# The value pass of a product-key expert layer, rewritten as one pipeline of columns with a pinned order

## The chip, the cores and the metric

One core of a Trainium2 chip runs one program. The metric is the device time of one execution in microseconds (us), taken as the median of several executions. The engines are TensorE (PE, with its weight loads shown apart as PEld), VectorE (DVE), ScalarE (ACT), GpSimd (POOL) and SyncE (SP). In this kernel nearly every transfer is issued by SP, from one queue, in the order in which the program puts them there.

## The reference, cut to what matters

The network has two layers. Each is a mixer (convolution, mLSTM and differential attention over 256 context and 256 latent tokens) followed by an expert layer with 16384 experts. The expert layer of a block of tokens is

```python
s = einsum(q(t), sub_keys); st, it = top_k(s, 16)          # two halves of the key
cand = st[..., 0, :, None] + st[..., 1, None, :]           # 16 x 16 sums, again top 16
g = softmax(best)                                          # gate of each chosen expert
u = take(eu, e, axis=0)
act = gelu(einsum("thkd,td->thk", u, t))
out = einsum("thk,thkd->td", g * act, take(ev, e, axis=0))
```

The kernel doesn't gather experts. It computes gelu(u t) for all 16384 experts, spreads the gates into a dense matrix G (zero for experts not chosen), and sums (G * act) times ev over all experts. The second half of that, the sum with ev, is the value pass.

## The kernel before, in words

The experts of a layer are 128 columns of 128. `peer` (L873) runs two phases. In the first, `route` finds and spreads the gates and writes them to DRAM (`G`), while `inner` (L851) computes the activations of a column: it loads `u`, splits it into a rounded part `uh` and a rest `ul`, runs the products on PE, takes the gelu (`ga`, L870) and stores that to DRAM (`act`). In layer 0 (512 tokens, so 512 activations per expert column and partition) all 128 columns are done there, since `NPRE[0]` is 128; in layer 1 (256 tokens) 104 of them are.

The second phase is `outer`, the value pass. Here is what one column of layer 0 costs:

- `weights` (L927): every fourth column loads the gate tile `g` (1 MB, L931) for four columns; every column loads its activations `gb` (256 KB, L937); DVE multiplies them (L943, in place), ACT rounds the product to `wh` (L946), DVE takes the rest `wl` (L947). It is called for two columns at a time.
- `values` (L952): loads the column's `v` (512 KB, L954); `usplit` splits it into two halves of `vh` (ACT, L846) and `vl` (DVE, L847).
- `second` (L957): 24 products of 128x128 by 128x512 on PE: for 4 blocks of 128 tokens and 2 halves of the 1024 outputs, `wh*vh` (L969), `wh*vl` (L970) and `wl*vh` (L971), summed over all columns in the 8 PSUM banks `acc`.
- one step of `side`, a generator that computes layer 1's modulation meanwhile: `wa` (512 KB, L177) is loaded every second column, and DVE multiplies it twice with a row-sum (`wtr`, L180).

The last column ends with `finish` (L975) for each bank: transposes, the residual and the statistics of the next norm, from which layer 1's front part follows.

What orders the work: the program is recorded and then a scheduler of the framework puts each engine's instructions, and SP's transfers, in an order of its own by its cost estimates; the semaphores follow from the buffers. A buffer of a tile name (its tag) is taken again only after everything that read it is done. The numbers of buffers for layer 0 are

```python
UB = (5, 8); UR = (2, 4)    # uh, ul: 5 each; u: 2
VB = (5, 6); VR = (2, 3)    # vh, vl: 5 each (halves of a column); v: 2
AB = (6, 4)                 # gb: 6;  wh, wl: 4 each;  g: 2;  wa: 2
```

Only the `wtr` steps are pinned (`keep_in_program_order`): pinned instructions of an engine keep the order in which the program names them, among themselves. All of PE's 3072 products of the value pass stand in the same order in any case, column by column.

The functions that the change touches, and what calls them:

Of the kernel before, what the change touches and what calls it, by code (L numbers as in the profile page):

```python
# [7 lines left out]
F32 = mybir.dt.float32  # L8
F32R = mybir.dt.float32r
# [3 lines left out]
AF = mybir.ActivationFunctionType  # L13
# [3 lines left out]
D = 1024  # L17
# [7 lines left out]
TG = 32  # L25
TT = 512
NPRE = (128, 104)
RATE = (((1, 3), (5, 8)), ((1, 2), (9, 8)))
UB = (5, 8)
UR = (2, 4)  # L30
VB = (5, 6)
VR = (2, 3)
AB = (6, 4)
# [17 lines left out]
class Net:  # L51
# [865 lines left out]
    def outer(self, l, P, h, c0, npre, Gd, Ad, pool, X, S, side):  # L917
        nc, I = self.nc, self.I
        n = TT - c0
        per = 512 // n  # L920
        nt = n // 128
        V = I["peer_v"][l].rearrange("(i j) d -> i j d", j=128)
        bank = lambda k: self.psum.tile([128, 512], F32, name=f"acc{k}", tag=f"acc{k}", bufs=1)
        acc = [bank(k) for k in range(2 * nt)]
        st = {}

        def weights(n2):  # L927

            if n2 % 2 == 0:
                st["g"] = X.tile([128, n // TG, 4, TG], F32, name="g", tag="g")  # L930
                nc.sync.dma_start(st["g"], Gd[:, :, 2 * n2:2 * n2 + 4, :])  # L931
            r = []
            for m in range(2 // per):
                bank = n2 * (2 // per) + m
                if bank * per < npre:
                    a = X.tile([128, 512], F32, name="gb", tag="gb", bufs=AB[l])
                    nc.sync.dma_start(a, Ad[bank])  # L937
                else:
                    a = st.pop(("a", bank))
                j4 = (bank * per) % 4  # L940
                av = a.rearrange("p (j a b) -> p j a b", j=per, b=TG)
                g = st["g"][:, :, j4:j4 + per, :].rearrange("p a j b -> p j a b")
                nc.vector.tensor_mul(av, av, g)  # L943
                wh = X.tile([128, 512], F32R, name="wh", tag="wh", bufs=2 * (2 // per))
                wl = X.tile([128, 512], F32R, name="wl", tag="wl", bufs=2 * (2 // per))
                nc.scalar.activation(wh, a, AF.Copy)  # L946
                nc.vector.tensor_sub(wl, a, wh)  # L947
                for k in range(per):
                    r.append((wh[:, k * n:(k + 1) * n], wl[:, k * n:(k + 1) * n]))
            st["w", n2] = r  # L950
# [6 lines left out]
        def second(n2):  # L957
            ws = st.pop(("w", n2))
            for jj in range(2):
                vs = values(2 * n2 + jj)  # L960
                wh, wl = ws[jj]
                s0, s1 = n2 == first and jj == 0, n2 == last and jj == 1
                order = (2, 0, 3, 1) if s1 and nt > 2 else range(nt)
                for tt in order:
                    t = slice(tt * 128, tt * 128 + 128)
                    for k in range(2):
                        A = acc[2 * tt + k]
                        vh, vl = vs[k]
                        nc.tensor.matmul(A, wh[:, t], vh, start=s0, stop=False)  # L969
                        nc.tensor.matmul(A, wh[:, t], vl, start=False, stop=False)  # L970
                        nc.tensor.matmul(A, wl[:, t], vh, start=False, stop=s1)  # L971
                        if s1:
                            finish(tt, k)
# [45 lines left out]
        early, late, seq = list(range(npre // 4)), list(range(npre // 4, 32)), []  # L1019
        for k in range(32):  # L1020
            q = late if not early or late and (k + 1) * (32 - npre // 4) // 32 > k * (32 - npre // 4) // 32 else early
            seq += [2 * q[0], 2 * q.pop(0) + 1]
        first, last = seq[0], seq[-1]
        for k in range(65):
            if k == 64:
                for _ in side:
                    pass
                self.log_exp(self.gelu)
            if k < 64:
                n2 = seq[k]  # L1030
                for j in (2 * n2, 2 * n2 + 1):
                    if j >= npre:
                        a = self.inner(l, h, c0, j, per, pool, S, nc.vector)
                        if a is not None:
                            st["a", j // per] = a
                weights(n2)
                next(side, None)
            if k:
                second(seq[k - 1])
            next(side, None)  # L1040


    def run(self):
# [110 lines left out]
```

## Time and profile before

| what | us |
|---|---|
| median of 3 executions (lowest to highest) | 3059.82 (3053.89 to 3063.95) |
| the profiled execution, its own time | 3061.33 |
| its span, first to last instruction | 3059.2 |
| TensorE busy / granted clock (share of full) | 2912.0 / 0.979 |
| VectorE, ScalarE, GpSimd busy | 2013.9, 1424.9, 1077.3 |
| value pass of layer 0, first product to the first product of its last column | 1227.3 to 1965.58 |

Times within the execution count from the first instruction of the span. A row of the view by groups gives line, engine, operation, tiles, count, busy time, mean ns, and the idle time of the engine just before with what ended it. A row of the view of waits gives who waited for whom, the total, how many times and the longest. Lines are those of the kernel before.

### The profile page before, as it was taken

To read this page: it belongs to the slowest core of one execution; us is meant where nothing else is said; L and a number is where in the kernel's file an instruction comes from. 1 tells how busy PE (TensorE), PEld (TensorE's weight loads), DVE (VectorE), ACT (ScalarE), POOL (GpSimd) and SP (SyncE) were. 2 spreads that over 40 slices of the span, in tenths; PEclk is the share of its full clock that TensorE was granted. 3 is DMA by queue.
4 is the path that set the end of the run, shared out by engine and by line. 5 is a ranking of instruction groups with operands and counts; after the bars stand their busy time and mean duration, and the time that the engine had idled before them with its cause. 6 is when DMAs were issued, how large, how long until landed. Compare 5 with 4: busy or idle time off the path is not lost.

```text
span 3059.2 us, 43325 instructions
## 1 busy us (share of the span) xinstructions
PE 2912.0 (95%) x14960; PEld 2407.3 (79%) x14960; DVE 2013.9 (66%) x4447; ACT 1424.9 (47%) x2862; POOL 1077.3 (35%) x887
## 2 busy tenths in 40 slices
PE   7899999999999999999999999988989999999998
PEld 4575578878888888887777777777689999888887
DVE  4856547865666665666665665486749788666665
ACT  4354443345665664332232223345455766555454
POOL 4333255656666665000000000054478877100000
PEclk9898899999999999999999999989999999999999
DMA  6521134445555556766766666221255877898773
GB/s 230 186 63 35 41 115 135 124 138 188 187 202 184 203 193 236 263 220 223 232 221 217 215 216 208 78 80 56 62 170 165 263 267 278 301 312 268 256 237 127
DMA packets 257868, 565.62 MB, mean 185 GB/s; under 512 B 18336, under 2 KB 119200, under 8 KB 254448
## 3 DMA queue, kind: packets, MB, share of 16 engines
q1 hardware_dynamic: 256928, 560.42, 54.5%
q8 instruction: 118, 1.93, 0.3%
q0 software_dynamic: 720, 2.43, 0.2%
q14 instruction: 102, 0.84, 0.1%
HBM read 464.21 MB, written 98.57 MB: 184 GB/s over the span
## 4 chain that ended last, share of the span: by engine, by line
PE 59%; DMA 13%; DVE 10%; issue 2%; ACT 2%; POOL 1%; SPq 0%; DVEq 0%; ACTq 0%; POOLq 0%
PE h L864 10%; PE h L866 10%; PE h L865 10%; DMA gb<-act 8%; PE acc L970 6%; PE acc L971 6%; PE acc L969 6%; DMA v<-in_peer_v 3%; PE f L813 3%; DVE vl L847 2%; DVE wl L947 1%; DVE cy L468 1%; PE f L311 1%; PE f L312 1%; DMA u<-in_peer_u 1%
## 5 line engine op out<-in xcount | busy, mean ns | idle before, releaser
L847 POOL TENSOR_TENSOR ul<-u,uh 128x512 fp32r<-128x512 f32 x464 | 611.6, 1328 | 335.4 <-ACT uh L846 317.3
L864 PE MATMUL h<-hh,uh 128*128 128x512 f32 (+1 forms) x2048 | 692.2, 338 | 3.8 <-ACT ga L870 3.8
L866 PE MATMUL h<-hh,ul 128*128 128x512 f32 (+1 forms) x2048 | 689.4, 337 | 5.2 <-POOL ul L847 5.1
L865 PE MATMUL h<-hl,uh 128*128 128x512 f32 (+1 forms) x2048 | 689.6, 337 | 0.0
L970 PE MATMUL acc<-vl,wh 128*128 128x512 f32 x1536 | 607.3, 396 | 28.6 <-DVE vl L847 27.5
L846 ACT ACTIVATE vh<-v 128x512 fp32r<-128x512 f32 x512 | 307.0, 626 | 660.9 <-DMA v<-in_peer_v 482.9
L969 PE MATMUL acc<-vh,wh 128*128 128x512 f32 x1536 | 598.5, 390 | 1.9 <-ACT vh L846 1.2
L971 PE MATMUL acc<-vh,wl 128*128 128x512 f32 x1536 | 599.2, 390 | 0.1
L846 ACT ACTIVATE uh<-u 128x512 fp32r<-128x512 f32 x512 | 319.1, 629 | 466.9 <-PE h L865 339.8
L847 DVE TENSOR_TENSOR vl<-v,vh 128x512 fp32r<-128x512 f32 x512 | 344.1, 687 | 171.4 <-ACT vh L846 171.0
L866 PEld LDWEIGHTS h<-hh,ul 128*128 128x128 f32 x2048 | 389.2, 190 | 47.1 <-POOL ul L847 6.3
L864 PEld LDWEIGHTS h<-hh,uh 128*128 128x128 f32 x2048 | 389.5, 190 | 45.2 <-ACT ga L870 5.7
L865 PEld LDWEIGHTS h<-hl,uh 128*128 128x128 f32 x2048 | 389.6, 190 | 37.0
L815 DVE TENSOR_REDUCE rt_stg<-f 128x256 f32<-128x512 f32 x384 | 245.0, 687 | 224.4 <-PE f L813 223.7
L970 PEld LDWEIGHTS acc<-vl,wh 128*128 128x128 f32 x1536 | 288.6, 188 | 114.9 <-DVE vl L847 57.3
L969 PEld LDWEIGHTS acc<-vh,wh 128*128 128x128 f32 x1536 | 288.8, 188 | 63.4 <-ACT vh L846 1.4
L971 PEld LDWEIGHTS acc<-vh,wl 128*128 128x128 f32 x1536 | 288.9, 188 | 58.2 <-DVE wl L947 0.6
L219 POOL TENSOR_TENSOR wlo<-wt,whi 128x512 fp32r<-128x512 f32 x164 | 231.4, 1422 | 253.4 <-ACT whi L218 230.1
L943 DVE TENSOR_TENSOR gb<-gb,g 128x512 f32<-128x512 f32 x180 | 126.0, 703 | 254.9 <-DMA gb<-act 252.2
L375 POOL MEMSET up<- 128x60 f32 (+1 forms) x2 | 0.3, 148 | 764.6 <-PE acc L991 764.6
L801 DVE SCALAR_TENSOR_TENSOR rt_oh_g<-iotap,rt_sT,rt_sg 128x256 fp32r<-128x256 f32 x512 | 213.4, 475 | 0.1
L218 ACT ACTIVATE whi<-wt 128x512 fp32r<-128x512 f32 x164 | 100.1, 626 | 140.6 <-PE f L298 52.2
(311 smaller groups left out, 4201.6 us busy)
## 6 DMA issues: line engine op xcount, KB each, us to landing
u<-in_peer_u SPq DMA_DIRECT2D x256, 512.0 KB, 4.0
v<-in_peer_v SPq DMA_DIRECT2D x256, 512.0 KB, 4.7
G<-rt_stg SPq DMA_DIRECT2D x24, 2048.0 KB, 6.7
act<-ga SPq DMA_DIRECT2D x180, 256.0 KB, 2.9
gb<-act SPq DMA_DIRECT2D x180, 256.0 KB, 4.8
g<-G SPq DMA_DIRECT2D x32, 1024.0 KB, 5.7
wa<-in_ada_t SPq DMA_DIRECT2D x56, 512.0 KB, 5.7
w<-in_ada_w SPq DMA_DIRECT2D x20, 1024.0 KB, 6.0
```

The costliest lines, as they stand in the source:

```text
L219: nc.gpsimd.tensor_sub(lo, raw, hi)
L801: nc.vector.scalar_tensor_tensor(og[:, k], self.iotap[:, None, :].to_broadcast([128, 2, 128]), sT[:, 1, c:c + 1], sg[:, c, :, None].bitcas ...
L815: nc.vector.tensor_reduce(stg[:, :, t4 + k2:t4 + k2 + 2].rearrange("p j t -> p t j"), pg.rearrange("p (t x j) -> p t j x", t=2, x=2), axis ...
L846: nc.scalar.activation(hi, raw[:, k * 512:(k + 1) * 512], AF.Copy)
L847: lo_eng.tensor_sub(lo, raw[:, k * 512:(k + 1) * 512], hi)
L864: nc.tensor.matmul(o, uh, hh[:, c, c0:], start=c == 0, stop=False)
L865: nc.tensor.matmul(o, uh, hl[:, c, c0:], start=False, stop=False)
L866: nc.tensor.matmul(o, ul, hh[:, c, c0:], start=False, stop=c == NB - 1)
L943: nc.vector.tensor_mul(av, av, g)
L969: nc.tensor.matmul(A, wh[:, t], vh, start=s0, stop=False)
L970: nc.tensor.matmul(A, wh[:, t], vl, start=False, stop=False)
L971: nc.tensor.matmul(A, wl[:, t], vh, start=False, stop=s1)
```

## The change

For layer 0 (`npre == 128`) `outer` now calls a new function, `outer_ahead`, and returns; layer 1 keeps the old code. The new function treats the 128 columns one by one. In the turn of column i it issues, in this order: the gate and activation loads of columns i+6 and i+7 (`gates`, every second turn), the load of v of column i+3 (`raw`), the split of column i+1 (`parts`), the rounding of the weights of column i+2 (`weight`), the gate product of column i+3 (`gated`), one step of `side`, and then the 24 products of column i. From the third turn on all of these but the products and the steps of `side` are pinned (the `wtr` of `side` were pinned before), so DVE, ACT and SP keep this order. v and its halves of odd columns live in the buffers of u, which are free by then, so there are 4 buffers of v where there were 2, and 10 each of vh and vl where there were 5. Counts of instructions, sizes and tiles of products are the same.

```diff
@@ -1021,6 +1021,9 @@
             q = late if not early or late and (k + 1) * (32 - npre // 4) // 32 > k * (32 - npre // 4) // 32 else early
             seq += [2 * q[0], 2 * q.pop(0) + 1]
         first, last = seq[0], seq[-1]
+        if npre == 128:
+            self.outer_ahead(l, seq, first, last, st, X, pool, Gd, Ad, V, acc, finish, side)
+            return
         for k in range(65):
             if k == 64:
                 for _ in side:
@@ -1038,6 +1041,105 @@
             if k:
                 second(seq[k - 1])
             next(side, None)
+
+    def outer_ahead(self, l, seq, first, last, st, X, pool, Gd, Ad, V, acc, finish, side):
+
+
+        nc = self.nc
+        cols = [2 * n2 + jj for n2 in seq for jj in range(2)]
+        hold = [False]
+
+        def pin(ins):
+            if hold[0]:
+                self.tc.keep_in_program_order(ins)
+            return ins
+
+        def gates(i):
+
+            if i >= len(seq):
+                return
+            n2 = seq[i]
+            if n2 % 2 == 0:
+                st["g", n2 // 2] = X.tile([128, TT // TG, 4, TG], F32, name="g", tag="g")
+                pin(nc.sync.dma_start(st["g", n2 // 2], Gd[:, :, 2 * n2:2 * n2 + 4, :]))
+            for j in (2 * n2, 2 * n2 + 1):
+                st["a", j] = X.tile([128, 512], F32, name="gb", tag="gb", bufs=AB[l])
+                pin(nc.sync.dma_start(st["a", j], Ad[j]))
+
+        def raw(i):
+            if i >= len(cols):
+                return
+            p, name = ((X, "v"), (pool, "u"))[i % 2]
+            v = st["v", i] = p.tile([128, D], F32, name="v", tag=name, bufs=(VR if i % 2 == 0 else UR)[l])
+            pin(nc.sync.dma_start(v, V[:, cols[i], :]))
+
+        def parts(i):
+            if i >= len(cols):
+                return
+            p, name, n = ((X, "v", VB), (pool, "u", UB))[i % 2]
+            v, r = st.pop(("v", i)), []
+            for k in range(2):
+                hi = p.tile([128, 512], F32R, name="vh", tag=name + "h", bufs=n[l])
+                lo = p.tile([128, 512], F32R, name="vl", tag=name + "l", bufs=n[l])
+                pin(nc.scalar.activation(hi, v[:, k * 512:(k + 1) * 512], AF.Copy))
+                pin(nc.vector.tensor_sub(lo, v[:, k * 512:(k + 1) * 512], hi))
+                r.append((hi, lo))
+            st["p", i] = r
+
+        def gated(i):
+
+            if i >= len(cols):
+                return
+            j = cols[i]
+            av = st["a", j].rearrange("p (a b) -> p a b", b=TG)
+            pin(nc.vector.tensor_mul(av, av, st["g", j // 4][:, :, j % 4, :]))
+
+        def weight(i):
+            if i >= len(cols):
+                return
+            a = st.pop(("a", cols[i]))
+            wh = X.tile([128, 512], F32R, name="wh", tag="wh", bufs=4)
+            wl = X.tile([128, 512], F32R, name="wl", tag="wl", bufs=4)
+            pin(nc.scalar.activation(wh, a, AF.Copy))
+            pin(nc.vector.tensor_sub(wl, a, wh))
+            st["w", i] = wh, wl
+
+        for i in range(3):
+            gates(i)
+            if i < 2:
+                raw(i)
+        raw(2)
+        gated(0)
+        gated(1)
+        weight(0)
+        parts(0)
+        gated(2)
+        weight(1)
+        for i in range(len(cols)):
+            hold[0] = i > 1
+            if i == len(cols) - 1:
+                for _ in side:
+                    pass
+                self.log_exp(self.gelu)
+            if i % 2 == 0:
+                gates(i // 2 + 3)
+            raw(i + 3)
+            parts(i + 1)
+            weight(i + 2)
+            gated(i + 3)
+            next(side, None)
+            (wh, wl), vs = st.pop(("w", i)), st.pop(("p", i))
+            s0, s1 = i == 0, i == len(cols) - 1
+            for tt in (2, 0, 3, 1) if s1 else range(4):
+                t = slice(tt * 128, tt * 128 + 128)
+                for k in range(2):
+                    A = acc[2 * tt + k]
+                    vh, vl = vs[k]
+                    nc.tensor.matmul(A, wh[:, t], vh, start=s0, stop=False)
+                    nc.tensor.matmul(A, wh[:, t], vl, start=False, stop=False)
+                    nc.tensor.matmul(A, wl[:, t], vh, start=False, stop=s1)
+                    if s1:
+                        finish(tt, k)
 
 
     def run(self):
```

VectorE, in the steady part of the pass. `gb` is a column's activations (number by buffer), `vl` the rest of v, `wl` the rest of the weights. First the kernel before, from the half split of one column to the gate product of a column six later than the first `wl` here (`gb_11899` takes the buffer that `wl_11635` frees by reading `gb_11631`):

```order
L847 TENSOR_TENSOR vl_11654<-v_11647,vh_11653 128x512
L947 TENSOR_TENSOR wl_11635<-gb_11631,wh_11634 128x512
L847 TENSOR_TENSOR vl_11684<-v_11681,vh_11683 128x512
L847 TENSOR_TENSOR vl_11688<-v_11681,vh_11687 128x512
L947 TENSOR_TENSOR wl_11642<-gb_11638,wh_11641 128x512
L180 SCALAR_TENSOR_TENSOR wtr_11645,red_11448<-wa_11627,cb_11440 128x1024
L180 SCALAR_TENSOR_TENSOR wtr_11717,red_11448<-wa_11715,cb_11440 128x1024
L847 TENSOR_TENSOR vl_11740<-v_11737,vh_11739 128x512
L943 TENSOR_TENSOR gb_11899<-gb_11899,g_11897 128x512
```

The same engine in the change, two turns of it (`gb_11650` takes the buffer of `gb_11440`, which was last read five turns before; `v_11695` takes the buffer of `v_11516`, split four turns before):

```order
L1095 TENSOR_TENSOR gb_11562<-gb_11562,g_11560 128x512
L180 SCALAR_TENSOR_TENSOR wtr_11712,red_11531<-wa_11710,cb_11484 128x1024
L1085 TENSOR_TENSOR vl_11747<-v_11654,vh_11746 128x512
L1085 TENSOR_TENSOR vl_11751<-v_11654,vh_11750 128x512
L1104 TENSOR_TENSOR wl_11755<-gb_11562,wh_11754 128x512
L1095 TENSOR_TENSOR gb_11564<-gb_11564,g_11560 128x512
L180 SCALAR_TENSOR_TENSOR wtr_11759,red_11531<-wa_11710,cb_11484 128x1024
L1085 TENSOR_TENSOR vl_11788<-v_11695,vh_11787 128x512
L1085 TENSOR_TENSOR vl_11792<-v_11695,vh_11791 128x512
L1104 TENSOR_TENSOR wl_11796<-gb_11564,wh_11795 128x512
L1095 TENSOR_TENSOR gb_11650<-gb_11650,g_11560 128x512
L180 SCALAR_TENSOR_TENSOR wtr_11802,red_11531<-wa_11800,cb_11484 128x1024
```

What moved: each turn is now split, split, `wl`, gate product, `wtr`, once each; before, gate products and `wtr` came in pairs between the splits. The gate product that stood seven rows behind the `wl` that frees its buffer now stands 26 rows behind it.

SP's transfers in the kernel before (`v_11771` takes the buffer of `v_11681`, two columns earlier):

```order
L954 DMA v_11737<-in_peer_v 128x1024
L937 DMA gb_11899<-act0_2986 128x512
L954 DMA v_11771<-in_peer_v 128x1024
L937 DMA gb_11906<-act0_2986 128x512
L177 DMA wa_11805<-in_ada_t 128x1024
L954 DMA v_11825<-in_peer_v 128x1024
L937 DMA gb_11987<-act0_2986 128x512
L954 DMA v_11859<-in_peer_v 128x1024
L937 DMA gb_11994<-act0_2986 128x512
```

SP's transfers in the change:

```order
L1067 DMA gb_11650<-act0_2986 128x512
L177 DMA wa_11710<-in_ada_t 128x1024
L1067 DMA gb_11652<-act0_2986 128x512
L1074 DMA v_11654<-in_peer_v 128x1024
L1074 DMA v_11695<-in_peer_v 128x1024
L1064 DMA g_11738<-G0_2985 128x16x128
L1067 DMA gb_11740<-act0_2986 128x512
L177 DMA wa_11800<-in_ada_t 128x1024
L1067 DMA gb_11742<-act0_2986 128x512
L1074 DMA v_11744<-in_peer_v 128x1024
```

What moved: the two `v` of a pair now stand together, behind the `gb` loads, four columns after the split that frees their buffers where it was two; `wa` and `g` keep their places between them.

ScalarE where the pass begins, in the kernel before (`uh` is the split of the last u columns, `ga` their gelu):

```order
L870 ACTIVATE ga_11288<-h_11255 128x512
L946 ACTIVATE wh_11429<-gb_11426 128x512
L946 ACTIVATE wh_11436<-gb_11433 128x512
L946 ACTIVATE wh_11456<-gb_11453 128x512
L846 ACTIVATE uh_11374<-u_11367 128x512
L846 ACTIVATE vh_11471<-v_11469 128x512
L846 ACTIVATE vh_11475<-v_11469 128x512
```

The same place in the change:

```order
L870 ACTIVATE ga_11288<-h_11255 128x512
L1103 ACTIVATE wh_11448<-gb_11426 128x512
L1103 ACTIVATE wh_11461<-gb_11428 128x512
L1084 ACTIVATE vh_11452<-v_11430 128x512
L1084 ACTIVATE vh_11456<-v_11430 128x512
L846 ACTIVATE uh_11374<-u_11367 128x512
L1103 ACTIVATE wh_11479<-gb_11432 128x512
```

What moved: the two halves of the first column of v come ahead of the last half of the last u (`uh_11374`). PE and POOL keep their order throughout, and on every engine the instructions of `finish` and those behind it stand in the same order in both. One `wtr` that the scheduler had put into the phase before (at 441.9 us) now stands in the pass.

## Rows read from the trace of the kernel before

**Rows 1.** Page: busy time of the engines; shares of the chain that ended last.

```profile
PE 2912.0 (95%) x14960; PEld 2407.3 (79%) x14960; DVE 2013.9 (66%) x4447; ACT 1424.9 (47%) x2862; POOL 1077.3 (35%) x887
PE 59%; DMA 13%; DVE 10%; issue 2%; ACT 2%; POOL 1%; SPq 0%; DVEq 0%; ACTq 0%; POOLq 0%
```

**Rows 2.** Two stretches, L970 alone: length, PE and PEld busy, clock, DMA share, GB/s.

```profile
1227.30:1379.70 152.40, 87.11 (x224) 42.04 (x224) 1.00 0.72 241
1379.70:1965.50 585.80, 317.30 (x793) 148.89 (x792) 1.00 0.62 207
```

**Rows 3.** The same stretches, all lines: length, PE, PEld, DVE, ACT, POOL.

```profile
1227.30:1379.70 152.40, 152.40 (x672) 126.02 (x673) 97.20 (x161) 48.76 (x83) 0.00 (x0) 1.00 0.72 241
1379.70:1965.50 585.80, 559.60 (x2378) 442.00 (x2377) 340.19 (x566) 167.10 (x298) 0.00 (x0) 1.00 0.62 207
```

**Rows 4.** Waits of the engines, 1227 to 1966 us.

```profile
ACT vh L846 <- DMA v<-in_peer_v: 418.4, 101, 9.3
DVE gb L943 <- DMA gb<-act: 174.4, 91, 4.7
DVE vl L847 <- ACT vh L846: 123.4, 42, 4.4
ACT vh L846 <- PE acc L971: 80.0, 34, 4.6
```

**Rows 5.** Waits of SP's queue, 1227 to 1966 us.

```profile
SPq L954 <- DVE vl L847: 341.3, 99, 6.1
SPq L931 <- DVE gb L943: 93.9, 28, 5.0
```

**Rows 6.** Timeline 1461 to 1473 us: SP, ACT, DVE, PE, some of the rows.

```profile
1463.76 0.33 SPq L954 DMA_DIRECT2D v<-in_peer_v  x1
1469.68 0.33 SPq L954 DMA_DIRECT2D v<-in_peer_v  x1
...
1467.77 1.15 ACT L846 ACTIVATE vh<-v 128x512 fp32r<-128x512 f32 x2 [4.27 <-DMA v<-in_peer_v]
...
1468.36 0.69 DVE L943 TENSOR_TENSOR gb<-gb,g 128x512 f32<-128x512 f32 x1 [3.42 <-DMA gb<-act]
1468.96 0.69 DVE L847 TENSOR_TENSOR vl<-v,vh 128x512 fp32r<-128x512 f32 x1
...
1469.71 0.50 PE L970 MATMUL acc<-vl,wh 128*128 128x512 f32 x1 [0.17 <-DVE vl L847]
```

**Rows 7.** Groups of DVE, 1227 to 1966 us; the last from the view of tile wa.

```profile
L847 DVE TENSOR_TENSOR vl<-v,vh 128x512 fp32r<-128x512 f32 x251 | 170.4, 687 | 123.4 <-ACT vh L846 123.4
L180 DVE SCALAR_TENSOR_TENSOR wtr<-wa,cb 128x1024 bf16<-128x1024 f32 x109 | 129.4, 1220 | 0.0
L947 DVE TENSOR_TENSOR wl<-gb,wh 128x512 fp32r<-128x512 f32 x124 | 84.9, 685 | 0.0
L943 DVE TENSOR_TENSOR gb<-gb,g 128x512 f32<-128x512 f32 x122 | 84.1, 691 | 174.6 <-DMA gb<-act 174.4
...
L180 DVE DVE_READ_ACCUMULATOR wtr<-wa,cb x112: 76/83/91, 443.1 to 1876.7; 128x1 f32 x112
```

**Rows 8.** DMA, 1227 to 1966 us: bytes, median landing; then extremes of v, of gb.

```profile
DMA packets 105463, 158.17 MB, mean 214 GB/s; under 512 B 5322, under 2 KB 66762, under 8 KB 105421
v<-in_peer_v SPq DMA_DIRECT2D x124, 512.0 KB, 5.0
gb<-act SPq DMA_DIRECT2D x120, 256.0 KB, 5.1
...
DMA to landing us min/median/max: 3.3/4.7/9.2
...
DMA to landing us min/median/max: 2.5/4.8/9.3
```

**Rows 9.** Timeline where the pass begins: ACT's last split of u, PE's first product.

```profile
1213.92 0.62 ACT L846 ACTIVATE uh<-u 128x512 fp32r<-128x512 f32 x1
...
1227.30 0.50 PE L969 MATMUL acc<-vh,wh 128*128 128x512 f32 x1 [0.74 <-ACT ga L870]
```

**Rows 10.** Page: the first write of layer 1's front into memory of the expert phase.

```profile
L375 POOL MEMSET up<- 128x60 f32 (+1 forms) x2 | 0.3, 148 | 764.6 <-PE acc L991 764.6
```

## The prediction

> **What bounds the kernel now.** I read the page first. TensorE is busy for 95% of the span and holds 59% of the chain that ended last [rows 1]. That is an average over stages, so it doesn't say whether the pass that is changed runs at TensorE's pace. For that I went to the table by stretches of the pass, for one line of products alone [rows 2]. L970 runs 8 times per column. In the first stretch 224 of them, 28 columns, take 152.4 us: 5.44 us a column. In the second, 792 of the 793 counted (99 whole columns; the last one that is counted starts at the edge) take 585.8 us: 5.92 us a column. The granted clock is 1.00, the full 2.4 GHz, in both. So the same 24 products have two paces in one pass, and the slow one costs 585.8 - 99 x 5.44 = 47 us.
>
> The reader should see here why "busy" would mislead. For all lines the second stretch shows TensorE busy 559.6 of 585.8 us [rows 3], which looks like 26 us to gain. But a product is drawn with its whole passage through the array, about 0.39 us, while the next one starts after 152.4/672 = 0.227 us. So every stall hides some 0.16 us behind the product before it. The pitch of the columns gives the true loss.
>
> Why the first stretch is clean: in it the splits wait for TensorE (ScalarE waits 80.0 us, 34 times, for the products L971 to free a buffer) [rows 4]. After it they wait for loads: ScalarE's `vh` 418.4 us for v, VectorE's gate product 174.4 us for `gb`, `vl` 123.4 us for `vh` [rows 4]. SP's queue shows the other end: it held a v load 341.3 us until a `vl` freed the buffer [rows 5]. That is a circle, and the timeline shows one turn of it [rows 6]: v is issued at 1463.76; ScalarE can split it at 1467.77; VectorE is meanwhile held 3.42 us by the gate product, runs it at 1468.36 and comes to the `vl` only at 1468.96; TensorE gets that at 1469.71; the buffer is free and the next v is issued at 1469.68. That turn is 5.92 us long, which is the mean pitch of these 99 columns. So the pass is bound by a circle of load, split and release that is a little longer than the 5.44 us of products, with VectorE's strict order making it longer.
>
> **The change part by part.** *Products:* number, size and order on TensorE are the same, so 5.44 us a column stays the floor. I take it from the clean stretch, 28 columns without a wait at the full clock [rows 2]. The Trainium skill (page "TensorE: Matmul & The Clock Gate", section "Back-to-back issue gap") gives N/2.4 + 2.5 ns for a warm product of N columns, 216 ns here; by that a column would be 5.18 us and the pass would have another 128 x 0.26 = 33 us to lose. The measured 227 ns differ from that and decide.
>
> *More buffers for v:* 4 in place of 2. A buffer is asked for again four columns later, so a circle has four columns of products, 21.8 us, to close in. Its parts in the trace are: the landing of a v load, median 5.0 us and at worst 9.2 [rows 8], two roundings (1.15 us in [rows 6]) and two rests (2 x 0.687 [rows 7]): 7.5 us, at worst 11.7, hence 1.9 to 2.9 us a column. In practice SP issues a pair of v behind a `gb` load that waits for a `wl`, in the turn of the split four columns back; the first v of the pair is needed after two more whole turns and the end of one, about 2 x 5.44 + 2 = 12.9 us, the second one turn later. The worst landing seen is still inside that.
>
> *Gate loads earlier:* the gate product is 26 rows behind the release of its buffer instead of seven. Before, the rows between are two `vl`, a `wl`, two `wtr` and another `vl`: 0.685 + 3 x 0.687 + 2 x (1.220 + 0.083) = 5.35 us of VectorE work [rows 7] against a landing of 5.1 us in the median plus its place in SP's queue [rows 8], which is why VectorE waited 91 times. Five turns of the new order are at least 20 us, at TensorE's pace 27 us, and the longest landing is 9.3 us [rows 8]. I put the wait at zero.
>
> *VectorE's own work* in a turn: 2 x 0.687 + 0.685 + 0.691 + 1.220 + 0.083 = 4.05 us [rows 7], against 5.44. There is room of 1.39 us. The added `wtr` (1.3 us, moved in from the phase before) is covered by it. ScalarE has three roundings a turn, at 1.15 us for two of them [rows 6]: under 2 us.
>
> *Transfers:* the same bytes. The pass moved 158 MB in 739 us, 214 GB/s [rows 8]; in 692 us it will be 229 GB/s. The clean stretch carried 241 GB/s with no stall [rows 2], so I cost this at nothing; the cover is the lead of two to six columns.
>
> *10 halves of vh and vl where there were 5:* the splits may run about two columns ahead of TensorE, so one late load no longer reaches it. Bounded below by nothing, above by the 47 us, already counted.
>
> *The start:* the last split of u comes behind two roundings of v, some 1.2 us later (it ran at 1213.92). The pass begins at 1227.30, so a delay of over 10 us would be needed to show; nothing. *The end:* the order from `finish` on is unchanged, and the front of layer 1 couldn't write into the memory of the expert phase before the transposes of `finish` either [rows 10], so keeping v in u's buffers delays nothing. The first product still waits for the last gelu, 0.74 us [rows 9].
>
> **The sum.** The profiled execution took 3061.3 us (span 3059.2, and 2.1 around it). Less 47 us: **3014 us**. It stood 1.5 us above the median of the runs shown, so against the median it is 3013. The ends: all 47 us gone and a run like the fastest shown, 3053.9 - 47 = 3007; a few stalls of the last columns or the change-over left, 8 us, 3022.
>
> **The rivals.**
>
> *A part stays.* The `g` load of every fourth column sits in the same queue and waited 93.9 us, 28 times, for a gate product [rows 5]; whatever stands behind it on SP, two v loads among it, waits too. For it: that order is kept. Against: those v loads have 13 us of lead and the longest hold was 5.0. If each of the 32 leaves a stall of 0.7 us on TensorE, 22 us stay: 3037 us.
>
> *Slower: VectorE sets the pace.* Pinning takes away the scheduler's freedom to put ready work ahead. If VectorE's waits stay as they are, (174.4 + 123.4)/128 = 2.33 us a column [rows 4], each turn is 4.05 + 2.33 = 6.38 us, over 112 turns with a `wtr` and 16 without (5.44): 802 us in place of 744, so 3061 + 58 = 3119 us. It decides when the waits exceed 1.39 us a turn. That takes landings beyond some 13 us, where the longest seen is 9.3. Deeper prefetch could lengthen them: the Trainium skill ("DMA: Bandwidth & Descriptors", section "Issuing engines are not separate DMA queues") says that all transfers interleave on the same 16 engines. The clean stretch, with a DMA share of 0.72 and no stall, speaks against.
>
> *It doesn't do what it says.* The loads stand early in the program, but SP issues them late, since each still waits for a release in order. Then the time is 3061 us. The order speaks against: the releases they wait for are four to six columns old.
>
> *The clean pitch falls too.* If the 5.44 us held small waits that the new order takes away, each 1% of it would give 7 us over the 128 columns, so 3007 us at 1% and 2979 us at 5%. Nothing in the clean stretch waits, which speaks against. (By the page's 216 ns it would be 5%, and 2981 us.)
>
> **How the numbers follow.** Forecast 0.82, a part stays 0.09, no change 0.04, slower 0.04, the clean pitch falls too 0.01. A measurement of this kernel can tell 0.3%, 9 us. Faster by over that: 0.82 + 0.09 + 0.01 = 0.92; same 0.04; slower 0.04. The forecast's own range is 3007 to 3022. It alone doesn't hold 8 in 10 with its own tails taken off, so the range reaches up to the case in which a part stays: 3006 to 3037.
>
> **What would show it.** In the profile after, the products of L970's successor should have one pitch, 5.44 us a column, over the whole pass, which ends (first product of the last column) near 1918 us instead of 1965.6. ScalarE's wait for v and VectorE's for `gb` should nearly vanish, and ScalarE should wait for the products (or VectorE for ScalarE's `wh`, which waits for them) as in the first stretch. SP should wait for releases that TensorE sets. The DMA rate in the pass should rise to about 229 GB/s. I am wrong if the pitch stays above 5.5 with VectorE waiting for `gb` or v, if VectorE shows no waits and the pitch follows its work, or if the pass shrinks and a later stage gives the time back.

## The result and the profile after

The changed kernel took 3006.61 us in the median (3002.47 to 3011.84, 4 executions), the kernel before 3057.0 us beside it (3053.89 to 3063.95, 4 executions). The ratio is 0.9842, with a 95% interval from 0.9815 to 0.9869: faster by 1.6%, and inside the range of the prediction. The profiled execution took 3002.47 us, its span is 3000.3 us. The new products stand on lines 1138 to 1140 of the changed kernel; L1084 and L1085 split v, L1095 is the gate product, L1103 and L1104 round the weights, L1067 loads `gb`, L1074 v and L1064 `g`.

The same two stretches of the pass as in [rows 2] and [rows 3], by length, from the table by stretches of the changed kernel: first the products of L1139 alone, then all lines of the second stretch.

```profile
1223.40:1375.70 152.30, 87.14 (x224) 42.04 (x224) 1.00 0.72 247
1375.70:1914.20 538.50, 308.03 (x793) 148.65 (x792) 1.00 0.66 224
...
1375.70:1914.20 538.50, 538.50 (x2378) 445.89 (x2377) 338.97 (x565) 164.75 (x295) 0.00 (x0) 1.00 0.66 224
```

The second stretch now takes 538.5 us for its 99 columns, 5.44 us each, the pace of the first; TensorE is drawn busy without a gap. From the first product to the first of the last column the pass takes 691.0 us where it took 738.3.

The views of waits in the pass, 1223 to 1915 us, engines first and then SP's queue; they answer to [rows 4] and [rows 5].

```profile
ACT wh L1103 <- PE acc L1139: 451.4, 120, 3.8
DVE wl L1104 <- ACT wh L1103: 236.2, 124, 2.9
ACT vh L1084 <- DMA v<-in_peer_v: 0.4, 1, 0.4
...
SPq L1067 <- DVE wl L1104: 284.7, 89, 5.0
SPq L1064 <- DVE gb L1095: 136.0, 29, 5.0
```

The wait of ScalarE for v is gone (418.4 us to 0.4), that of VectorE for `gb` has no row left. The long waits now lead back to TensorE: ScalarE waits 120 times for the products to free a `wh`, VectorE for ScalarE, SP for VectorE. On the page the chain that ended last has lost its DMA (13% in [rows 1]):

```profile
PE 76%; DVE 7%; DMA 1%; POOL 1%; ACT 1%; issue 1%; SPq 0%; DVEq 0%; ACTq 0%; POOLq 0%
```

VectorE's gate product, with no idle time ahead of it, and the transfers in the pass, as in [rows 7] and [rows 8]:

```profile
L1095 DVE TENSOR_TENSOR gb<-gb,g 128x512 f32<-128x512 f32 x123 | 84.1, 684 | 0.0
...
DMA packets 105353, 158.24 MB, mean 229 GB/s; under 512 B 5307, under 2 KB 66747, under 8 KB 105313
v<-in_peer_v SPq DMA_DIRECT2D x123, 512.0 KB, 5.2
gb<-act SPq DMA_DIRECT2D x120, 256.0 KB, 3.4
```

Nearly the same bytes in less time, 229 GB/s; hardly anything waits for them.

The two profiles differ by 58.9 us, of which the pass is 47.3. The pass begins 4.0 us earlier and what follows it is 7.6 us shorter. Over all the profiles of this study the pass begins between 1212.1 and 1227.3 us and what follows its last column takes between 1085.2 and 1097.3 us, in kernels of either kind, so I put these parts down to executions that differ.

### The profile page after: what moved, and what is told of

Same layout as the page of the kernel before. It is cut to its first block, busy times and chain, and to the rows that moved or that the text cites. A ratio compares the mean times of both kernels' runs of the same rounds, so it can differ in the third digit from the quotient of the medians.

```text
span 3000.3 us, 43088 instructions
## 1 busy us (share of the span) xinstructions
PE 2884.3 (96%) x14960; PEld 2409.7 (80%) x14960; DVE 2009.4 (67%) x4447; ACT 1422.2 (47%) x2862; POOL 1075.4 (36%) x887
## 4 chain that ended last, share of the span: by engine, by line
PE 76%; DVE 7%; DMA 1%; POOL 1%; ACT 1%; issue 1%; SPq 0%; DVEq 0%; ACTq 0%; POOLq 0%
PE h L864 10%; PE h L865 10%; PE h L866 10%; PE acc L1138 8%; PE acc L1139 8%; PE acc L1140 8%; PE acc L969 4%; PE acc L970 4%; PE acc L971 4%; PE f L813 3%; DVE cy L468 1%; PE f L311 1%; PE f L312 1%; PE f L313 1%; DMA v<-in_peer_v 1%
## 5 line engine op out<-in xcount | busy, mean ns | idle before, releaser
L1139 PE MATMUL acc<-vl,wh 128*128 128x512 f32 x1024 | 398.6, 389 | 0.0
L1140 PE MATMUL acc<-vh,wl 128*128 128x512 f32 x1024 | 398.5, 389 | 0.0
L1103 ACT ACTIVATE wh<-gb 128x512 fp32r<-128x512 f32 x128 | 80.7, 632 | 463.3 <-PE acc L1139 451.4
L1104 DVE TENSOR_TENSOR wl<-gb,wh 128x512 fp32r<-128x512 f32 x128 | 88.8, 695 | 236.9 <-ACT wh L1103 236.8
L1138 PEld LDWEIGHTS acc<-vh,wh 128*128 128x128 f32 x1024 | 192.2, 188 | 41.4 <-ACT ga L870 1.5
L1140 PEld LDWEIGHTS acc<-vh,wl 128*128 128x128 f32 x1024 | 192.2, 188 | 39.8
L1139 PEld LDWEIGHTS acc<-vl,wh 128*128 128x128 f32 x1024 | 192.2, 188 | 39.7
L846 ACT ACTIVATE vh<-v 128x512 fp32r<-128x512 f32 x256 | 155.7, 626 | 140.8 <-PE acc L971 81.4
```

The source lines that it names most:

```text
L846: nc.scalar.activation(hi, raw[:, k * 512:(k + 1) * 512], AF.Copy)
```

## The experiments

The length of the pass (first product to first product of the last column) is read from each profile; a column is a 127th of it. It is the sharper measure, since the total of one kernel varies by 10 us and more. Each ratio is to the kernel before as it ran beside that experiment, where its median was 3054.3 to 3066.5 us.

| run | pass, us | a column, us | median total, us | ratio to before, 95% interval |
|---|---|---|---|---|
| before | 738.3 | 5.81 | 3057.0 | 1 |
| before_again | 746.6 | 5.88 | 3069.9 (one run) | |
| changed | 691.0 | 5.44 | 3006.6 | 0.9842, 0.9815 to 0.9869 |
| again | 693.8 | 5.46 | 3001.0 | 0.9791, 0.9756 to 0.9825 |
| old_borrow | 717.5 | 5.65 | 3034.0 | 0.9905, 0.9871 to 0.9938 |
| new_nopin | 721.9 | 5.68 | 3039.8 | 0.9918, 0.9894 to 0.9943 |
| new_v2_h5 | 692.3 | 5.45 | 3005.6 | 0.9803, 0.9759 to 0.9846 |
| order_gate1 | 691.0 | 5.44 | 3004.3 | 0.9794, 0.9745 to 0.9843 |
| new_dve2 | 691.0 | 5.44 | 3008.8 (one run) | |
| new_dve3 | 715.3 | 5.63 | 3031.6 (one run) | |
| circle | 845.6 | 6.66 | 3156.9 | 1.0344, 1.0303 to 1.0384 |
| circle_flip | 691.0 | 5.44 | 3008.0 | 0.9843, 0.9818 to 0.9869 |
| old_gbpool | 878.8 | 6.92 | 3193.4 | 1.0449, 1.0419 to 1.048 |

**How much of it is the pass.** `again` is the changed kernel, `before_again` the kernel before.

> The changed kernel once more, to settle how much of its gain lies in the value pass of layer 0. If the 47 us of stalls in that pass are all there is, the ratio to the kernel before is 0.9846 (3010 us against 3057), the pass from its first product to the first of the last column takes 691 us, and the start of the pass and the stages behind it differ from one execution to the next by some us without a pattern. If the change also shortens other stages (the profiles showed 4.0 us ahead of the pass and 7.7 us behind it), those show again and the ratio is near 0.981.

> The kernel before, a second profile. If its pass is about as long as in the first (738 us, within some 5 us), the changed kernel's gain in the pass is about 47 us and what is more in the medians lies in stages that differ from execution to execution. If the pass of the kernel before is itself uneven (745 us or more), the gain of the pass is larger than the first profile said.

`again` gave 0.9791, its pass 693.8 us; the interval leaves out the 0.9846 of the first expectation and holds the 0.981 of the second. But the second profile of the kernel before has a pass of 746.6 us, 8 us longer than the first, as the second expectation of `before_again` had it. So the stalls of the kernel before are themselves uneven, and the pass gains 44 to 56 us from profile to profile. Whether a few us more lie elsewhere the runs don't settle; the starts and ends show no pattern that goes with the kernel.

**Buffers or order.** Three kernels. `old_borrow` gives the old code the buffers alone:

```diff
         def values(j):
+            if l == 0 and j % 2:
+                v = pool.tile([128, D], F32, name="v", tag="u", bufs=UR[l])
+                nc.sync.dma_start(v, V[:, j, :])
+                return self.usplit(v, "u", pool, UB[l], nc.vector)
             v = X.tile([128, D], F32, name="v", tag="v", bufs=VR[l])
```

> The kernel before, with only the buffers of the change: odd columns of v use u's buffers, so 4 of v and 10 each of vh and vl; the scheduler keeps its freedom. Theory of the v buffers (the circle of load, split and release is what costs): the pass falls from 738 us to 691 to 700 us, ratio 0.985. Theory of the gate product's place (VectorE waits for gb in front of a ready split): the gate products still stand close behind the release of their buffers, so VectorE still waits for gb and the pass stays above 720 us, ratio 0.993 or more.

`new_v2_h5` is the change with the old number of buffers:

```diff
-            p, name = ((X, "v"), (pool, "u"))[i % 2]
-            v = st["v", i] = p.tile([128, D], F32, name="v", tag=name, bufs=(VR if i % 2 == 0 else UR)[l])
+            p, name = X, "v"
+            v = st["v", i] = p.tile([128, D], F32, name="v", tag=name, bufs=VR[l])
...
-            p, name, n = ((X, "v", VB), (pool, "u", UB))[i % 2]
+            p, name, n = X, "v", VB
...
-        raw(2)
...
-            raw(i + 3)
+            raw(i + 2)
```

> The change with the buffers of before: 2 of v, 5 each of vh and vl, v loaded two columns ahead in the program where it was three; the pinned order and the early gates stay. Theory of the v buffers: the circle is back, the pass is 720 us or more and ScalarE waits for v more than 200 us. Theory of the gate product's place: with the gate product 26 rows behind the release the rest is fast enough, the pass is 691 to 700 us.

`new_nopin` is the change without its pins:

```diff
-            hold[0] = i > 1
+            hold[0] = False
```

> The change with no instruction pinned (but the wtr, as before): buffers and program order of the change, the scheduler decides. If buffers and lead in the program suffice, the pass is 691 to 695 us. If the pinned order is what counts, VectorE again waits for gb (over 100 us in the pass) and the pass is 705 to 738 us.

The old buffers with the new order give the whole gain (692.3 us); the new buffers with the scheduler's order give a third to a half of it (717.5 and 721.9 us). For `old_borrow` that lies between its two expectations (691 to 700, above 720), and neither is met. The waits in the pass of `new_v2_h5`:

```profile
ACT vh L1084 <- PE acc L1139: 409.7, 125, 5.2
ACT vh L1084 <- DMA v<-in_peer_v: 55.1, 36, 2.7
```

and of `new_nopin`:

```profile
ACT vh L1084 <- DMA v<-in_peer_v: 326.1, 85, 9.6
DVE gb L1095 <- DMA gb<-act: 254.9, 113, 4.1
...
PEld acc L1140 <- DVE wl L1104: 34.6, 53, 2.5
```

With two buffers of v in the new order ScalarE waits for v 55 us in all, for TensorE 410. Without the pins VectorE waits 254.9 us for `gb`, more than in the kernel before, and now the late piece is `wl`. So the theory that the number of v buffers is what costs falls. What was left were two: the place of the gate product close behind the release of its buffer, or simply an uneven order.

**The gate product's place.** `order_gate1` is `new_v2_h5` with the gate products moved to one turn behind the release of their buffers; `gates` loads one column at a time there, and more of them ahead of the first turn:

```diff
-            if i % 2 == 0:
-                gates(i // 2 + 3)
...
-            gated(i + 3)
+            gates(i + 8)
+            for _ in range(2):
+                if nxt <= i + 7:
+                    gated(nxt)
+                    nxt += 1
```

> As new_v2_h5 (pinned order, 2 buffers of v, 5 each of vh and vl), but each gate product stands one turn behind the release of its buffer (five rows of VectorE, 4.05 us of work), as close as it stood before the change, and so six columns ahead of its use where it was one. Theory of the gate product's place: VectorE waits for gb again, 100 us or more in the pass, and the pass grows by 15 us or more over the 692 us of new_v2_h5. Theory of the even order (what counts is that splits and rests alternate evenly): the pass stays within 5 us of 692.

691.0 us, and the wait is hardly there:

```profile
DVE gb L1093 <- DMA gb<-act: 3.6, 6, 1.7
```

So that theory falls too: the five rows, in a turn of 5.44 us, are enough for a load that nothing else holds.

**VectorE's room.** The rest of the weights computed three and four times:

```diff
-            pin(nc.vector.tensor_sub(wl, a, wh))
+            for _ in range(3):
+                pin(nc.vector.tensor_sub(wl, a, wh))
```

> The change with the rest of the weights computed three times in each turn instead of once, so VectorE has 4.05 + 2 x 0.69 = 5.43 us of work a turn. If VectorE's room of 1.39 us a turn is real, the pass stays at 691 to 697 us. If it has less room (waits that its place in the queue brings), the pass is 700 us or more.

> The same with the rest computed four times: 6.12 us of work a turn, beyond the 5.44 us of the products. VectorE sets the pace in the 112 turns with a wtr: 112 x 6.12 + 15 x 5.5 = 768 us for the pass if the order costs nothing further. If TensorE set the pace all the same, 691 us.

Two more rests a turn cost nothing (691.0 us), three cost 24 us (715.3), a column of 5.63 us. The first is as expected; the second stays 53 us under the 768 that I had worked out from durations. The timeline of the changed kernel says why (start, length; an idle time ahead of it in brackets):

```profile
1463.50 0.69 DVE L1104 TENSOR_TENSOR wl<-gb,wh 128x512 fp32r<-128x512 f32 x1 [1.80 <-ACT wh L1103]
1464.11 0.68 DVE L1095 TENSOR_TENSOR gb<-gb,g 128x512 f32<-128x512 f32 x1
1464.71 1.22 DVE L180 SCALAR_TENSOR_TENSOR wtr<-wa,cb 128x1024 bf16<-128x1024 f32 x1
...
1465.86 1.29 DVE L1085 TENSOR_TENSOR vl<-v,vh 128x512 fp32r<-128x512 f32 x2
1468.94 0.69 DVE L1104 TENSOR_TENSOR wl<-gb,wh 128x512 fp32r<-128x512 f32 x1 [1.79 <-ACT wh L1103]
```

An instruction of 0.69 us is followed by the next after 0.60 or 0.61 us. A turn of 5.44 us has 1.80 us of waiting, so its work is 3.64 us, where the sum of durations says 4.05. A repeated rest, which writes the same `wl` again, comes dearer. In `new_dve3` the four of a turn end 2.86 us after the first starts, so they start (2.86 - 0.69)/3 = 0.72 us apart:

```profile
1642.99 2.86 DVE L1105 TENSOR_TENSOR wl<-gb,wh 128x512 fp32r<-128x512 f32 x4
...
1648.72 2.87 DVE L1105 TENSOR_TENSOR wl<-gb,wh 128x512 fp32r<-128x512 f32 x4
```

From one turn to the next it is 5.73 us, without idle time on VectorE: it sets the pace there. The mean of 5.63 is lower because most of the first 36 columns and the last ones, which have no `wtr`, keep 5.44.

**The circle through two queues.** I then read the timeline of the kernel before again, with the `gb` loads in it. These rows belong to the stretch of [rows 6]:

```profile
1464.36 0.33 SPq L937 DMA_DIRECT2D gb<-act  x1
1470.28 0.33 SPq L937 DMA_DIRECT2D gb<-act  x1
...
1464.25 0.68 DVE L847 TENSOR_TENSOR vl<-v,vh 128x512 fp32r<-128x512 f32 x1
```

`gb` is issued at 1464.36. The gate product waits for it and starts at 1468.36, 4.0 us later. The second half of a split stands behind that product and starts at 1468.96; its first half ran at 1464.25, so it belongs to the column before the v that landed at 1467.7. Its end frees a buffer, SP issues v at 1469.68, and only behind that, 0.60 us later, the next `gb` at 1470.28. 4.0 + 0.60 + 0.72 + 0.60 = 5.92 us: that is one turn of the circle. It runs through the gate product and SP's queue, not through the landing of v.

That this turn is as long as the mean column of the slow stretch is chance. The v loads around the two of [rows 6], issued by SP:

```profile
1454.60 0.49 SPq L954 DMA_DIRECT2D v<-in_peer_v  x1
...
1475.44 1.34 SPq L954 DMA_DIRECT2D v<-in_peer_v  x1
1477.35 0.52 SPq L954 DMA_DIRECT2D v<-in_peer_v  x1
```

From 1454.60 over 1463.76, 1469.68 and 1475.44 to 1477.35 the steps are 9.16, 5.92, 5.76 and 1.91 us, and much the same four return through most of the slow stretch. In the long one `gb`, issued at 1455.18 behind `g` and two v, lands only at 1462.34; in the short one both halves of a split stand together. So the circle closes in about three columns of four: counted over the pass, 88 of 123 v loads are issued within 0.3 us of the end of a `vl` directly behind a gate product that had waited for a `gb` issued after the v load before (none in the changed kernel). Two kernels put it to the test. `circle` has the pinned order and the buffers of `new_v2_h5`, with the circle put back (the turn is shown against that kernel; `parts` splits one half and `gates` loads one column there, and more loads stand ahead of the first turn):

```diff
-            if i % 2 == 0:
-                gates(i // 2 + 3)
-            raw(i + 2)
-            parts(i + 1)
+            parts(i + 1, 0)
+            gated(i + 6)
+            parts(i + 1, 1)
+            raw(i + 3)
+            gates(i + 7)
             weight(i + 2)
-            gated(i + 3)
```

> New theory, the circle through two queues: in the kernel before, a gb load stands behind a v load on SP; that v load waits for the second half of a split on VectorE; that half stands behind a gate product; and the gate product waits for the gb load before. One turn is 4.0 us of gb load, 0.6 of product, 0.7 of half split and 0.6 of issuing v, 5.9 us, the pitch of the slow columns. This kernel has the pinned, even order and the buffers of new_v2_h5 (2 of v, 5 each of vh and vl) with that circle put back in: in each turn half a split, the gate product, the other half; on SP v ahead of gb. Theory of the circle: about 5.9 us a column, the pass 735 to 760 us. Theory of the even order (a pinned, regular order is enough): 691 to 697 us.

`circle_flip` exchanges two transfers and nothing else:

```diff
-            raw(i + 3)
             gates(i + 7)
+            raw(i + 3)
```

> The same, and only the two transfers of a turn change places on SP: gb ahead of v. Theory of the circle: gb's load then waits for nothing of the same turn, the circle is open, the pass is 691 to 697 us though VectorE's order is that of the run circle. Theory that the gate product between two halves of a split is what costs: as long as circle.

845.6 against 691.0 us, 3157 against 3008 in the median, from two transfers that change places. In `circle` 119 of 123 v loads close the circle. Timeline of `circle`, SP first, then VectorE:

```profile
1607.80 0.33 SPq L1072 DMA_DIRECT2D v<-in_peer_v  x1
1608.17 0.42 SPq L1065 DMA_DIRECT2D gb<-act  x1
1613.46 0.33 SPq L1072 DMA_DIRECT2D v<-in_peer_v  x1
...
1607.08 0.69 DVE L1081 TENSOR_TENSOR vl<-v,vh 128x512 fp32r<-128x512 f32 x1
1612.13 0.69 DVE L1090 TENSOR_TENSOR gb<-gb,g 128x512 f32<-128x512 f32 x1 [2.02 <-DMA gb<-act]
1612.74 0.69 DVE L1081 TENSOR_TENSOR vl<-v,vh 128x512 fp32r<-128x512 f32 x1
```

One turn, from v at 1607.80 to v at 1613.46, is 5.66 us and made of the same links. The waits in the pass, `circle` first, then `circle_flip`:

```profile
DVE gb L1090 <- DMA gb<-act: 385.0, 119, 7.7
SPq L1072 <- DVE vl L1081: 534.7, 123, 6.6
...
DVE gb L1090 <- DMA gb<-act: 36.1, 29, 3.7
SPq L1072 <- DVE vl L1081: 398.1, 124, 5.0
```

In `circle_flip` SP's v loads still wait 398 us for a split, and VectorE has the same uneven place of the gate product; but `gb` is no longer behind v, and the wait of the gate product falls from 385 to 36 us. So the theory of the even order falls as well, since `circle` is as even as can be. My size for `circle` was too small (735 to 760): I had left out `g`. Every fourth turn its 1 MB stands between v and `gb`:

```profile
1598.05 0.33 SPq L1072 DMA_DIRECT2D v<-in_peer_v  x1
1598.42 0.52 SPq L1063 DMA_DIRECT2D g<-G  x1
1599.28 3.29 SPq L1065 DMA_DIRECT2D gb<-act  x1
...
1606.47 0.69 DVE L1090 TENSOR_TENSOR gb<-gb,g 128x512 f32<-128x512 f32 x1 [6.10 <-DMA gb<-act]
```

From v at 1598.05 to v at 1607.80 it is 9.75 us; three turns of 5.66 and one of 9.75 make 6.68 us a column, against 6.66 measured. The granted clock of the whole pass also fell, to 0.95.

**The old code with `gb` on another queue.** One edit to the kernel before:

```diff
-                    nc.sync.dma_start(a, Ad[bank])
+                    (nc.sync if l else nc.gpsimd).dma_start(a, Ad[bank])
```

> The kernel before with one edit: the gb loads of layer 0 are issued by GpSimd's queue, which is idle in the pass, so no v load stands ahead of them. Theory of the circle: the pass falls from 738 to 747 us to 691 to 705 us, ratio 0.982 to 0.987, without any pinned order or more buffers. Theory of the even order: the scheduler's order is still uneven (gate products between half splits, wtr in pairs), the pass stays above 725 us. It may also lose some us to the slower issue of that queue.

The expectation of the circle missed; that of the even order (above 725 us) holds as a bound, but not for its reason: 878.8 us, the slowest of all. The waits, GpSimd's queue included:

```profile
POOL gb L937 <- DVE wl L947: 769.1, 117, 13.8
DVE gb L943 <- DMA gb<-act: 248.3, 89, 5.4
```

The scheduler put the instructions in a new order with this edit. The gate product now stands two rows behind the `wl` that frees its buffer (it was seven):

```order
L947 TENSOR_TENSOR wl_11813<-gb_11809,wh_11812 128x512
L847 TENSOR_TENSOR vl_11862<-v_11859,vh_11861 128x512
L943 TENSOR_TENSOR gb_12077<-gb_12077,g_12075 128x512
L847 TENSOR_TENSOR vl_11866<-v_11859,vh_11865 128x512
L947 TENSOR_TENSOR wl_11820<-gb_11816,wh_11819 128x512
```

So a load lies between `wl` and a gate product that stand almost side by side, and the next `wl` stands behind that product: another circle, through one queue less. Timeline of that kernel, GpSimd's issues and VectorE:

```profile
1604.72 0.55 POOL L937 DMA_DIRECT2D gb<-act  x1 [6.68 <-DVE wl L947]
1610.60 0.55 POOL L937 DMA_DIRECT2D gb<-act  x1 [5.33 <-DVE wl L947]
...
1608.41 0.70 DVE L943 TENSOR_TENSOR gb<-gb,g 128x512 f32<-128x512 f32 x1 [3.38 <-DMA gb<-act]
1609.62 0.68 DVE L947 TENSOR_TENSOR wl<-gb,wh 128x512 fp32r<-128x512 f32 x1
```

The load issued at 1604.72 brings the product at 1608.41, `wl` follows at 1609.62, the next load at 1610.60: 5.88 us, plus the `wtr` in every second turn. A cleaner test, the old order with `gb` ahead of v on SP, wasn't tried: that the circle cost the kernel before its 47 us is read from its trace and from `circle` and `circle_flip`, not from an edit to it. In `old_borrow` (244.6 us of waiting for `gb` on VectorE) the same circle still closes, for 59 of 122 v loads. In `new_nopin` it closes for 10 only; what holds that kernel at 721.9 us stays open.

## Why the prediction was right, point by point

**The size.** The 47 us of stalls went: 47.3 us in the first pair of profiles, 44 to 56 over all pairs. The floor of 5.44 us a column, taken from the clean stretch, held for the whole pass, in `order_gate1`, `new_dve2` and `circle_flip` too, and no run showed a lower pitch, so the clean pitch did not fall. The total came out 7 us under the forecast (3006.6 against 3014), within what start and end of the pass vary by, and only 0.6 us above the low end of the range. `again`, the same kernel, has a median of 3001.0 us, below it: that the total fell inside owes something to luck, the size of the pass does not.

**The signs to look for.** The pass ended (first product of its last column) at 1914.3 us, having begun 4.0 us early (1918 forecast); the waits for v and `gb` vanished, ScalarE waits for the products, the DMA rate is 229 GB/s, as written. `finish`, the start and layer 1 gave nothing back.

**"Why the first stretch is clean".** It wasn't. The waits that I gave to the time after it are those of the whole pass, and part of them falls into the first stretch (1227.3 to 1379.7 us):

```profile
ACT vh L846 <- PE acc L971: 51.6, 21, 3.9
ACT vh L846 <- DMA v<-in_peer_v: 47.2, 21, 6.9
DVE gb L943 <- DMA gb<-act: 33.2, 20, 3.4
```

Only TensorE had no wait there, and the circle turned already, for 18 of 25 v loads. TensorE lived on a lead: the last `vl` of the third column ended at 1233.8 and its first product started at 1238.3, some 4.6 us later; at the 25th column, which started at 1358.0, that lead was gone (1358.2). The 5.44 us stood even so, since they are TensorE's own pace.

**"That is a circle".** Right that the slow columns turn in a circle, and that one turn of it takes 5.92 us; wrong in which circle, and in taking that turn for the mean pitch, which four unequal steps make. I took the `vl` at 1468.96 for the split of the v issued at 1463.76 and let the circle run through the landing of v, with the gate product an aggravation. It is the second half of the column before. The links are gate product, half split, release, v in SP's queue ahead of `gb`, `gb`, gate product. I had held the row of the v loads in SP's queue (341.3 us, [rows 5]) against the landing of v, and didn't look at what is queued behind those held loads: the `gb` loads.

**"More buffers for v".** Costed as one of the reasons; with the new order two buffers and five halves do as well (692.3 us), and the buffers without the order (`old_borrow`) give 21 to 29 of the 44 to 56 us.

**"Gate loads earlier".** Right that the wait goes to zero, wrong in why: five rows behind the release do as well as 26 (691.0 us). I had set 5.35 us of VectorE's work against a landing of 5.1 us "plus its place in SP's queue", and that place is what decided.

**"VectorE's own work".** The term was mis-sized: 3.64 us a turn, not 4.05, since durations overlap. The room is 1.8 us, not 1.39. It was covered either way: `new_dve2` adds two rests of 0.72 us and loses nothing.

**The rivals.** Of "a part stays" nothing showed: SP's `g` loads were held longer than before (136.0 us), and TensorE had no gap. "VectorE sets the pace" has a relative in `circle`: a pinned order that is slower, 3157 us, where I had worked out 3119; that the two are near is chance. What decides is not landings beyond 13 us, as I wrote; in `circle` the median landing of `gb` is 4.1 us. What decides is which transfer stands ahead of which on SP. The Trainium skill ("DMA: Bandwidth & Descriptors", section "Issuing engines are not separate DMA queues") has all transfers interleave on the same 16 engines; the runs show no harm from that with the deeper prefetch (landing of v 5.0 to 5.2 us, of `gb` 5.1 to 3.4). The 216 ns of the Trainium skill ("TensorE: Matmul & The Clock Gate", section "Back-to-back issue gap"), which that section gives for an isolated product and I took for the pitch of a stream, were reached in no run of this pass; 0.227 us remains.

## What to carry to other kernels

Where an engine is neither full nor waiting for the bottleneck, follow one of its waits all the way round, through the queue that issues the load: what stands ahead of that load there, and what that one waits for. Count how often such a circle closes, and don't trust one turn that happens to equal the mean pitch. If it closes within one step, changing the order of two transfers can be worth more than doubling buffers (here 155 us between `circle` and `circle_flip`, 21 to 29 us for the buffers), and an order that is left to a scheduler can close another one after the smallest edit. A stretch in which the busiest engine doesn't wait may still be running down a lead.

## What the runs showed of the hardware that was not expected

Two VectorE instructions in a row start 0.60 to 0.61 us apart though each is drawn 0.69 us long, and the 1.22 us of a `wtr` with the 0.08 us read of its sum are followed after 1.15 us: sums of durations overstate VectorE's load by some 11% here. Rests that write the same tile one after another start 0.72 us apart (`new_dve2`, `new_dve3`). The pitch of the products, 0.227 us, was the same at 224 and at 247 GB/s, and with two more rests a turn on VectorE (`new_dve2`), which leave it 0.35 us idle in a turn where it had 1.80.
